# Where the early tiles of the FFN's `rest` lie, and where HGRN's modulation steps stand

## The chip, the cores and the metric

The kernel runs on one core of a Trainium2 chip. The metric is the device time of one execution in microseconds (us), the median of several runs. The engines are TensorE (PE in the profile; its weight loads are PEld), VectorE (DVE), ScalarE (ACT), GpSimd (POOL) and SyncE (SP, whose queue issues nearly all DMAs). Each engine works through its own instructions in a fixed order, and waits where an instruction's inputs or buffers are not ready.

## The reference, cut to what matters

A backbone of two layers on 512 latent tokens with 1024 features and 256 context tokens. Each layer is a half-step SwiGLU, a token mixer, and another half-step SwiGLU; each of these is modulated ahead and normalised behind:

```python
def modulate(x, m, k):
    return x * (1 + m[..., 3 * k + 1, :]) + m[..., 3 * k, :]
def post_norm_update(x, y, m, k, g, b):
    return layer_norm(DN_ALPHA * x + m[..., 3 * k + 2, :] * y, g, b)
def swiglu(h, w_in, w_out):
    gate, up = jnp.split(h @ w_in, 2, axis=-1)
    return (jax.nn.silu(gate) * up) @ w_out
```

The vectors m come from `silu(cond) @ w_mod + b_mod`, nine rows of 1024 for each layer. Layer 0's mixer is a bidirectional HGRN2 with 8 heads of 128: per head and direction a forget gate, a cumulative sum of its logarithm, scores inside chunks, states carried between chunks from the context's final state, and then `o * rsqrt(mean(o*o) + eps) * norm_w * silu(g)`, which goes to the output projection. Layer 1's mixer is a chunked spatial-gating MLP (CM).

## The kernel before, in words

**Matmuls.** Every fp32 operand is held as a high and a low part: `split` copies the high part on ScalarE (L136) and subtracts on VectorE (L137). `mm3` makes one product of three matmuls, high·high, high·low, low·high (L149 to L151). `unit` loads one block of weights (tile raw, three buffers, DMA on SP) and splits it into a tile w (six buffers).

**Stages.** f0 and f1 are the first FFN on latent and context tokens. Then come HGRN's values and heads (641 to 977 us in the trace), its output phase, f2 (second FFN of layer 0), f3 (first FFN of layer 1), CM, f4 (second FFN of layer 1) and the last output phase. An output phase (`OutPhase`) multiplies into y, and at the end of the stage makes the new x: it adds y times a gate row (L305, L307), takes statistics and normalises (L310, L315, L329; GpSimd makes the root, rstd), transposes x on PE (tile pt), scales it into the next stage's operand (L351) and splits that into xm. Between this and the first product of the next stage lies what is called the boundary here. Meanwhile it multiplies x by its norm weights (L296, L297; rows rg and rb from DRAM) and stores x to DRAM (L298); the next output phase loads it again (L360).

**f2, f3, f4.** `FeedSums` computes the two input halves of a SwiGLU block by a scheme with seven products on half-size operands in place of eight, on sums of operand parts (f5, f6, f4, f7) and of weight parts. `rest` runs over 20 blocks of 128 hidden features, in the order psc, pse, psc, psa, psc, pse, psc (banks in PSUM; 84 matmuls in each block). For each block it loads two weight blocks, raw and rawu (L561, L563), forms the weight sums e and changed rawu and raw by L572, L573, L574 and L576, splits the four, multiplies, keeps partial results in sc (ScalarE, L584), and combines them (L599 to L604). The first product needs only the split of raw; the second, into pse, needs e. The first blocks of f2, f3 and f4 are made during the boundary's tail from earlier units (psf; L485), and the rest in this loop.

**Where tiles lie.** Pools are opened and closed like a stack on the on-chip memory (SBUF). A tile that lies on bytes of a closed pool waits for the last readers and writers of the tiles that lay there before. So the place of a tile sets how early its DMA or its first instruction can be.

**HGRN.** For head h the order in the source is: forget gate of direction 0 (`proj_forget`: projections psfl and psfc, then a chain on VectorE and ScalarE that ends with Q, L890), the previous head's output transposes (`gated`: pto, L998, then ht, L1000), key transposes and scores of head h−1, forget gate of direction 1, states of head h−1 (S, Sc; L944 to L968), query projection (psq), and `outputs` of head h−1: product po from Sc and scores, squares (on), reduction to ss (L987, L988), a power on GpSimd (rs, L990), and on2 (L992), which the next `gated` transposes. Then the gate projection g.

**Modulation steps.** The 32 steps that make four rows of layer 1's modulation are spread through HGRN. A step loads 512 KB (tile mraw, two buffers, SP, L177) and multiplies it by the conditioning row in two instructions on VectorE (tile junk, L171), each with a read of its accumulator; after eight steps a reduction (L184) ends a row. `mod_step(n)` emits n steps, each with an edge that keeps it behind the instruction that `latest[0]` holds, which before is always the last split. A scheduler then orders each engine's instructions by its own estimates, within what the data and such edges allow.

Of the kernel before, what the change touches and what calls it, by code (L numbers as in the profile page):

```python
# [18 lines left out]
P = 128  # L19
D = 1024  # L20
# [50 lines left out]
def backbone_kernel(  # L71
# [433 lines left out]
    class FeedSums(FeedIn):  # L505
# [32 lines left out]
            add(self.f6, (1, 2), (0, 0))  # L538
            add(self.f7, (0, 2), (1, 2))

        def rest(self, hp, nmod=0):
            for f in range(len(self.pss) // 2):
                self.evac(hp, self.pss[2 * f], self.pss[2 * f + 1])
            K2, N2 = D // 2, 2 * P
            lo, hi = slice(0, K2), slice(K2, D)
            xm = self.xm
            b11, b21, b22 = (
                xm[:, :, k0 : k0 + KD // 2, c0 : c0 + N2] for k0, c0 in ((0, 0), (KD // 2, 0), (KD // 2, N2))
            )

            def product(ps, w, c0, b, start, stop):
                for k in range(KD // 2):
                    c = slice(c0 + k * P, c0 + (k + 1) * P)
                    mm3(
                        ps[:, :N2], (w[:, 0, c], w[:, 1, c]), (b[:, 0, k, :], b[:, 1, k, :]),
                        start and k == 0, stop and k == KD // 2 - 1, skip_group_check=True,
                    )

            for f in range(len(self.hs), NF):
                g = wpool.tile([P, D], F32, tag="raw", name="raw", bufs=3)  # L560
                nc.sync.dma_start(g, self.src(2 * f))  # L561
                u = hp.tile([P, D], F32, tag="rawu", name="rawu", bufs=2)
                nc.sync.dma_start(u, self.src(2 * f + 1))  # L563
                e = hp.tile([P, D], F32, tag="e", name="e", bufs=2)

                def weights(src, n=D):
                    w = wpool.tile([P, 2, D], F32R, tag="w", name="w", bufs=6)
                    split(w[:, 0, :n], w[:, 1, :n], src[:, :n])
                    return w

                wg = weights(g)
                nc.vector.tensor_tensor(e[:, lo], g[:, lo], u[:, lo], ALU.subtract)  # L572
                nc.vector.tensor_tensor(u[:, lo], u[:, hi], u[:, lo], ALU.subtract)  # L573
                nc.vector.scalar_tensor_tensor(e[:, hi], u[:, lo], -1.0, g[:, lo], ALU.mult, ALU.subtract)  # L574
                we = weights(e)
                nc.vector.scalar_tensor_tensor(g[:, lo], g[:, hi], -1.0, e[:, hi], ALU.mult, ALU.subtract)  # L576
                wu = weights(u)
                w4 = weights(g, K2)

                pc, pe, pa = bank("psc"), bank("pse"), bank("psa")  # L580
                sc = hp.tile([P, 4, N2], F32, tag="sc", name="sc", bufs=2)

                def kept(i, ps, scale=1.0):
                    nc.scalar.activation(sc[:, i, :], ps[:, :N2], AF.Copy, scale=scale)  # L584

                product(pc, wg, 0, b11, True, True)
                kept(0, pc)
                product(pe, we, 0, self.f5, True, True)
                kept(1, pe)
                product(pc, we, K2, self.f6, False, True)  # L590
                kept(2, pc)
                product(pa, wg, K2, b21, True, True)
                product(pc, wu, 0, self.f4, False, True)
                kept(3, pc, -1.0)
                product(pe, wu, K2, self.f7, False, True)
                product(pc, w4, 0, b22, False, True)
                s = hp.tile([P, T], F32, tag="silu", name="silu", bufs=1)
                h = hp.tile([P, T], F32, tag="h", name="h", bufs=NF)
                nc.vector.tensor_tensor(s[:, :N2], pa[:, :N2], sc[:, 0, :], ALU.add)  # L599
                nc.scalar.activation(s[:, :N2], s[:, :N2], AF.Silu)  # L600
                nc.vector.tensor_tensor(h[:, N2:], sc[:, 3, :], sc[:, 1, :], ALU.subtract)
                nc.vector.tensor_tensor(h[:, :N2], pe[:, :N2], sc[:, 2, :], ALU.add)
                nc.scalar.activation(s[:, N2:], pc[:, :N2], AF.Silu, scale=-1.0)
                nc.vector.tensor_tensor(h, h, s, ALU.mult)  # L604
                self.hs.append(h)
                mod_step(nmod)
                next(self.later, None)
            for _ in self.later:
                pass
            self.place.close()  # L610
            return lambda k: self.hs[k]
# [141 lines left out]
    with sbuf(name="hgo", bufs=1) as hgo, ExitStack() as late:  # L753
# [14 lines left out]
        with sbuf(name="hg", bufs=1) as hg:  # L768
# [81 lines left out]
            def proj_forget(h, d):  # L850
# [36 lines left out]
                    nc.vector.scalar_tensor_tensor(X3[:, s, :], B3[:, s, :], ref, X3[:, s, :], ALU.subtract, ALU.add)  # L887
                nc.scalar.activation(X, X, AF.Exp, scale=-1.0, bias=lnoml[:, i : i + 1])
                Q = B3[:, :NT, :]
                nc.vector.tensor_tensor(Q, Q, sm[:, :NT].unsqueeze(2).broadcast_to([P, NT, P]), ALU.subtract)  # L890
                nc.scalar.activation(Q, Q, AF.Exp)
                r.kk, r.Q, r.d = X3, Q, d
                return r, last
# [79 lines left out]
            def outputs(h, dirs):  # L973
# [15 lines left out]
                rs = hg.tile([P, NT, 1], F32, tag="rs", name="rs", bufs=2)  # L989
                nc.gpsimd.tensor_tensor(rs[:, :, 0], ss, neghalf[:, :NT], ALU.pow)  # L990
                on2 = hg.tile([P, NT, P], F32, tag="tmp", name="on2", bufs=3)
                nc.vector.tensor_tensor(on2, po3, rs.broadcast_to([P, NT, P]), ALU.mult)  # L992
                return on2

            def gated(h, on, g):
# [13 lines left out]
            for h in range(NH + 1):  # L1009
                if h == NH - NLATE + 2:  # L1010
                    late_outputs()
                mod_step(2 if h else 0)
                if h < NH:
                    n0, last = proj_forget(h, 0)
                else:
# [9 lines left out]
                    far_scores(0, r0)  # L1025
                if h == NH and 0 == 1:
                    gated(*done)
                mod_step(2 if h else 0)
                if h < NH:
                    n1, _ = proj_forget(h, 1)  # L1030
                if prev:
                    context_states(h - 1, prev, kTc)
                    kT1 = transposed([r1.kk[:, s, :] for s in lat_order(1)[:-1]])
                    latent_states(h - 1, 0, r0, kT0)
                    far_scores(1, r1)
                    latent_states(h - 1, 1, r1, kT1)
# [4 lines left out]
                else:  # L1041
                    if 0 == 2:
                        gated(*done)
                    op.lead(0, 2)
                mod_step(3 if h else 0)
                if prev:
                    on = outputs(h - 1, prev)
                    g, last = proj_silu(h - 1, 3, "g")
                    done = (h - 1, on, g)
                if h < NH:  # L1050
# [9 lines left out]
    L0.close()  # L1060


    with sbuf(name="hp2", bufs=1) as hp, bpools() as bp:
        hget = f2.rest(hp)
        xm = new_xm(xmp, "xm", T)
        f3 = FeedSums(
            1, 0, xm, NT,
# [5 lines left out]
        )  # L1073
        op.nhs = 8
        op.run(bp)
        hget = f3.rest(hp)
        xm = new_xm(xmp, "xm", T)

        class GateIn(Phase):
# [32 lines left out]
    with ExitStack() as vhp_stack:  # L1112
        vhp = vhp_stack.enter_context(sbuf(name="vh", bufs=NG + 1))
        hs = []
        bp = vhp_stack.enter_context(bpools())
        bw = []

        def new_block(i):
            if i % 3 == 0:
                bw.append(vhp.tile([P, NT, GC], F32, tag="vh", name="bw").rearrange("p t c -> p (t c)"))  # L1120
            return bw[-1][:, i % 3 * T : (i % 3 + 1) * T].rearrange("p (k t) -> p k t", k=2)

        f4 = FeedSums(1, 1, None, NT, new_block)
        op = OutPhase(
            lambda k: hs[k // 3][:, k % 3, :], CI // P, lambda hf, kk: cm_w_out[hf, kk], NT, 1, 1, "x", 1.0,
            lambda t: x4[t], True, (1, 2), None, lambda t: x5[t], f4, tail=3,
# [74 lines left out]
                hs.append(ht)  # L1201
        xm = new_xm(xmp, "xm", T)
        f4.xm = op.xm = xm
        op.run(bp)

    with sbuf(name="hp4", bufs=1) as hp, bpools() as bp:
        hget = f4.rest(hp)
        OutPhase(
            hget, NF, ffn_units(1, 1), NT, 1, 2, "x", 0.5, lambda t: x5[t], True, None,
            None, lambda t: out[t], None, tail=4,  # L1210
# [79 lines left out]
```

## Time and profile before

| | us |
|---|---|
| median of 3 runs | 2551.97 |
| lowest and highest | 2549.63, 2554.30 |
| the profiled execution's own time | 2548.07 |
| span of the profiled execution | 2546.4 |
| PE busy | 2449.6 (96%) |
| VectorE busy | 1887.0 (74%) |
| ScalarE busy | 1099.0 (43%) |
| mean granted PE clock | 0.987 of full speed |

How rows are read: in a timeline row stand the start, the duration, the engine, the line, the operation, out<-in, shapes and a count; brackets hold the idle time just before it and what ended it. A row of waits holds the total, the number and the longest. A row of windows holds the stretch, its length, busy time of PE, PEld, VectorE, ScalarE and GpSimd with the number of instructions, the granted PE clock, the share of DMA time and GB/s. SPq is SP's queue of DMA issues.

### The profile page before, as it was taken

The numbers are of one execution on the slowest core, as the hardware profiler recorded it, in microseconds if no ns is written. First come the engines' busy times: TensorE is split into PE (matmuls) and PEld (weight loads), VectorE is DVE, ScalarE is ACT, GpSimd is POOL, SyncE is SP. The second block draws the span as 40 slices with busy tenths as digits, with TensorE's granted clock in tenths as the row PEclk, the third lists the DMA queues.
The fourth block names the chain that finished last, engine by engine and source line by source line (L and its number), as shares of the span: only waits on it lengthen the run. The fifth ranks groups of instructions, "written<-read, shape, count | busy, mean of one in ns | idle before, by whom it ended". The sixth has DMA issues, their size and how long they took to land.

```text
span 2546.4 us, 37450 instructions
## 1 busy us (share of the span) xinstructions
PE 2449.6 (96%) x14687; PEld 2201.0 (86%) x14687; DVE 1887.0 (74%) x3361; ACT 1099.0 (43%) x1671; POOL 49.0 (2%) x82
## 2 busy tenths in 40 slices
PE   7999999999999999699999999998999999799998
PEld 5888889978888888699988999888998888699987
DVE  7965479783899986788756988657786346888765
ACT  4222434453444452455633555533332243455642
POOL 0000000000000000000000000000010000000001
PEclk9999999999999999899999999999999999899999
DMA  8866357973434213423432532325863223333332
GB/s 322 292 196 199 95 170 247 317 252 111 149 115 126 92 60 107 153 100 103 135 103 67 172 111 100 116 93 170 304 194 108 83 91 95 131 105 102 115 100 79
DMA packets 111170, 368.06 MB, mean 145 GB/s; under 512 B 12760, under 2 KB 16016, under 8 KB 110992
## 3 DMA queue, kind: packets, MB, share of 16 engines
q1 hardware_dynamic: 110992, 365.65, 43.3%
q8 instruction: 115, 1.88, 0.3%
q14 instruction: 63, 0.52, 0.1%
HBM read 352.99 MB, written 12.61 MB: 144 GB/s over the span
## 4 chain that ended last, share of the span: by engine, by line
PE 70%; DVE 17%; DMA 6%; ACT 3%; issue 2%; POOL 1%; SPq 0%; POOLq 0%; DVEq 0%; ACTq 0%
PE y L151 7%; PE y L150 7%; PE y L149 7%; PE psc L149 4%; PE psc L151 4%; PE psc L150 4%; PE psf L150 3%; PE psf L151 3%; PE psf L149 3%; DMA raw<-in_ffn_w_in 2%; DVE w L137 2%; PE pse L149 2%; PE pse L151 2%; PE pse L150 2%; DVE junk L171 2%
## 5 line engine op out<-in xcount | busy, mean ns | idle before, releaser
L137 DVE TENSOR_TENSOR w<-raw,w 128x1024 fp32r<-128x1024 f32 (+1 forms) x458 | 517.1, 1133 | 176.8 <-ACT w L136 175.0
L136 ACT ACTIVATE w<-raw 128x1024 fp32r<-128x1024 f32 (+1 forms) x458 | 449.9, 984 | 382.8 <-PE y L151 91.3
L149 PE MATMUL y<-w,hs 128*128 128x512 f32 x984 | 384.7, 391 | 2.3 <-ACT hs L136 2.2
L151 PE MATMUL y<-w,hs 128*128 128x512 f32 x984 | 384.4, 391 | 2.4 <-DVE hs L137 2.4
L150 PE MATMUL y<-w,hs 128*128 128x512 f32 x984 | 383.8, 390 | 0.0
L137 DVE TENSOR_TENSOR hs<-h,hs 128x512 fp32r<-128x512 f32 (+1 forms) x220 | 136.3, 636 | 151.6 <-ACT hs L136 151.6
L136 ACT ACTIVATE hs<-h 128x512 fp32r<-128x512 f32 (+1 forms) x220 | 126.1, 587 | 240.7 <-PE y L151 231.2
L151 PEld LDWEIGHTS y<-w,hs 128*128 128x128 f32 x984 | 185.2, 188 | 43.5 <-DVE hs L137 5.5
L149 PEld LDWEIGHTS y<-w,hs 128*128 128x128 f32 x984 | 185.2, 188 | 43.1 <-ACT hs L136 4.8
L150 PEld LDWEIGHTS y<-w,hs 128*128 128x128 f32 x984 | 185.1, 188 | 38.1
L149 PE MATMUL psf<-xm,w 128*128 128x512 f32 (+1 forms) x544 | 192.3, 360 | 19.8 <-ACT xm L136 19.3
L151 PE MATMUL psf<-xm,w 128*128 128x512 f32 (+1 forms) x544 | 193.6, 357 | 2.1 <-DVE w L137 2.1
L150 PE MATMUL psf<-xm,w 128*128 128x512 f32 (+1 forms) x544 | 194.1, 357 | 0.8 <-DVE xm L137 0.8
L171 DVE SCALAR_TENSOR_TENSOR junk<-mraw,srow_x 128x512 bf16<-128x512 f32 x256 | 167.0, 686 | 12.1 <-DMA mraw<-in_mod_w 11.9
L149 PE MATMUL pse<-f,w 128*128 128x256 f32 x480 | 137.3, 286 | 35.9 <-ACT w L136 35.9
L149 PE MATMUL psc<-f,w 128*128 128x256 f32 x480 | 136.9, 285 | 0.7 <-ACT sc L584 0.7
L151 PE MATMUL psc<-xm,w 128*128 128x256 f32 x480 | 136.1, 284 | 1.3 <-DVE w L137 1.3
L151 PE MATMUL pse<-f,w 128*128 128x256 f32 x480 | 137.3, 286 | 0.0
L150 PE MATMUL pse<-f,w 128*128 128x256 f32 x480 | 137.0, 285 | 0.0
L150 PE MATMUL psc<-f,w 128*128 128x256 f32 x480 | 136.5, 284 | 0.0
L151 PE MATMUL psc<-f,w 128*128 128x256 f32 x480 | 136.4, 284 | 0.0
L149 PE MATMUL psc<-xm,w 128*128 128x256 f32 x480 | 135.9, 283 | 0.0
(259 smaller groups left out, 5926.8 us busy)
## 6 DMA issues: line engine op xcount, KB each, us to landing
raw<-in_ffn_w_in SPq DMA_DIRECT2D x160, 512.0 KB, 4.5
mraw<-in_mod_w SPq DMA_DIRECT2D x144, 512.0 KB, 4.6
raw<-in_ffn_w_out SPq DMA_DIRECT2D x110, 512.0 KB, 3.6
rawu<-in_ffn_w_in SPq DMA_DIRECT2D x60, 512.0 KB, 3.5
raw<-in_hg_wf SPq DMA_DIRECT2D x32, 512.0 KB, 4.2
raw<-in_cm_wv SPq DMA_DIRECT2D x32, 384.0 KB, 4.0
raw<-in_cm_wu SPq DMA_DIRECT2D x24, 512.0 KB, 3.7
raw<-in_cm_w_out SPq DMA_DIRECT2D x24, 512.0 KB, 3.5
```

The costliest lines, as they stand in the source:

```text
L136: nc.scalar.activation(dst_hi, src, AF.Copy)
L137: latest[0] = nc.vector.tensor_tensor(dst_lo, src, dst_hi.bitcast(F32), ALU.subtract)
L149: nc.tensor.matmul(ps, ah, bh, start=start, stop=False, **kw)
L150: nc.tensor.matmul(ps, ah, bl, start=False, stop=False, **kw)
L151: return nc.tensor.matmul(ps, al, bh, start=False, stop=stop, **kw)
L171: nc.vector.scalar_tensor_tensor(junk, w[:, c], 1.0, s[:, c], ALU.mult, ALU.mult, dst[:, i : i + 1])
```

## The change

It has two parts.

First, `rest` takes rawu, e and sc (24 KB in all) from a pool of their own, sp2 for f2 and f3 and sp4 for f4, which is opened ahead of hp2 and hp4 and so lies lower in the stack. At f2 these bytes belonged to xmc, the context operand (rawu and e), and to the first heads' output tiles (sc); at f4 to buffers of CM's gate values. Before, the three lay behind silu and h in hp, on the output phase's x, t1 and row tiles and on the blocks bw. The blocks of f4 come from a new pool, bw4, in place of spare buffers of vh.

Second, in HGRN `latest[0]` is also set to Q's subtraction (L890) and to on2 (L992), and the steps of a head stand at two places: two behind the forget gate of direction 1, five behind `outputs`. Before they stood at three places (two, two and three), ahead of the forget gates and of `outputs`, and the edge was to the last split.

```diff
-        def rest(self, hp, nmod=0):
+        def rest(self, hp, sp, nmod=0):
...
-                u = hp.tile([P, D], F32, tag="rawu", name="rawu", bufs=2)
+                u = sp.tile([P, D], F32, tag="rawu", name="rawu", bufs=2)
...
-                e = hp.tile([P, D], F32, tag="e", name="e", bufs=2)
+                e = sp.tile([P, D], F32, tag="e", name="e", bufs=2)
...
-                sc = hp.tile([P, 4, N2], F32, tag="sc", name="sc", bufs=2)
+                sc = sp.tile([P, 4, N2], F32, tag="sc", name="sc", bufs=2)
...
-                nc.vector.tensor_tensor(Q, Q, sm[:, :NT].unsqueeze(2).broadcast_to([P, NT, P]), ALU.subtract)
+                latest[0] = nc.vector.tensor_tensor(Q, Q, sm[:, :NT].unsqueeze(2).broadcast_to([P, NT, P]), ALU.subtract)
...
-                nc.vector.tensor_tensor(on2, po3, rs.broadcast_to([P, NT, P]), ALU.mult)
+                latest[0] = nc.vector.tensor_tensor(on2, po3, rs.broadcast_to([P, NT, P]), ALU.mult)
...
             for h in range(NH + 1):
                 if h == NH - NLATE + 2:
                     late_outputs()
-                mod_step(2 if h else 0)
                 if h < NH:
                     n0, last = proj_forget(h, 0)
...
-                mod_step(2 if h else 0)
                 if h < NH:
                     n1, _ = proj_forget(h, 1)
+                mod_step(2 if h else 0)
...
-                mod_step(3 if h else 0)
                 if prev:
                     on = outputs(h - 1, prev)
+                    mod_step(5)
                     g, last = proj_silu(h - 1, 3, "g")
...
-    with sbuf(name="hp2", bufs=1) as hp, bpools() as bp:
-        hget = f2.rest(hp)
+    with sbuf(name="sp2", bufs=1) as sp, sbuf(name="hp2", bufs=1) as hp, bpools() as bp:
+        hget = f2.rest(hp, sp)
...
-        hget = f3.rest(hp)
+        hget = f3.rest(hp, sp)
...
-        f4 = FeedSums(1, 1, None, NT, new_block)
+        f4 = FeedSums(1, 1, None, NT, lambda i: bw.tile([P, 2, 2 * P], F32, name=f"bw{i}"))
...
+        bw = vhp_stack.enter_context(sbuf(name="bw4", bufs=1))
         op.run(bp)
 
-    with sbuf(name="hp4", bufs=1) as hp, bpools() as bp:
-        hget = f4.rest(hp)
+    with sbuf(name="sp4", bufs=1) as sp, sbuf(name="hp4", bufs=1) as hp, bpools() as bp:
+        hget = f4.rest(hp, sp)
```

What this does to the order of instructions is shown at three places. In the rows stand the line, the operation, out<-in and the shape.

SP's queue at the start of f2, before and of the change as one difference (x_84 is the store of x to DRAM; gr_8_x the gate row that the output phase behind f2 will use):

```order
 L234 DMA rgate<-gr_5_x 128x512
+L563 DMA rawu<-in_ffn_w_in 128x1024 x2
 L561 DMA raw<-in_ffn_w_in 128x1024
 L234 DMA rgate<-gr_8_x 128x512
-L298 DMA x_84<-x 128x512
-L234 DMA rg<-in_ln_g 128x512
-L234 DMA rb<-in_ln_b 128x512
-L298 DMA x_84<-x 128x512 x3
```

The first two loads of rawu stood behind eight stores of x and two loads of it; they now stand behind the second gate row of the phase before.

VectorE in the first evacuations and norms of the same boundary, as one difference:

```order
 L305 SCALAR_TENSOR_TENSOR t_9213<-y_9061,rgate 128x512
+L572 TENSOR_TENSOR e<-raw,rawu 128x512
 L307 TENSOR_TENSOR x<-x,t_9213 128x512
+L573 TENSOR_TENSOR rawu<-rawu 128x512
-L310 BN_STATS st<-x 128x6
-L315 BN_AGGR mv<-st 128x2
+L310 BN_STATS st<-x 128x6
+L305 SCALAR_TENSOR_TENSOR t_9224<-y_9062,rgate 128x512
+L315 BN_AGGR mv<-st 128x2
+L574 SCALAR_TENSOR_TENSOR e<-rawu,raw 128x512
 L329 TENSOR_SCALAR x<-x,mv,rstd 128x1024
```

The steps that form e, which stood behind the whole boundary, now stand between the evacuations that the first norms wait for; a second pair (L572, L573) follows before the second norm, and the split of e stands in the middle of the operand splits.

VectorE in HGRN around on2 of the fourth head; before:

```order
L831 TENSOR_TENSOR g_7603<-psq_7578,g_7603 128x512
L861 TENSOR_SCALAR X_7677<-psfl_7625 128x512
L137 TENSOR_TENSOR w_8009<-raw_8007,w_8009 128x1024
L171 SCALAR_TENSOR_TENSOR junk_7610,acc_x_7338<-mraw_7608,srow_x_5500 128x512
L171 SCALAR_TENSOR_TENSOR junk_7612,acc_x_7338<-mraw_7608,srow_x_5500 128x512
L987 TENSOR_REDUCE ss_7566<-on_7564 128x4
L171 SCALAR_TENSOR_TENSOR junk_7616,acc_x_7338<-mraw_7614,srow_x_5500 128x512
L988 TENSOR_SCALAR ss_7566<-ss_7566 128x4
L171 SCALAR_TENSOR_TENSOR junk_7618,acc_x_7338<-mraw_7614,srow_x_5500 128x512
L992 TENSOR_TENSOR on2_7571<-po_7551,rs_7569 128x512
```

And of the change, one head later, around on2 of the fifth:

```order
L831 TENSOR_TENSOR g_7993<-psq_7968,g_7993 128x512
L968 SCALAR_TENSOR_TENSOR S_7879<-pkl_7863,se_7385,S_7879 128x128
L137 TENSOR_TENSOR w_8009<-raw_8007,w_8009 128x1024
L962 TENSOR_SCALAR Sc_7882<-S_7879,se_7385 128x128
L137 TENSOR_TENSOR w_8126<-raw_8124,w_8126 128x1024
L137 TENSOR_TENSOR w_8273<-raw_8271,w_8273 128x1024
L137 TENSOR_TENSOR w_8336<-raw_8334,w_8336 128x1024
L987 TENSOR_REDUCE ss_7940<-on_7938 128x4
L988 TENSOR_SCALAR ss_7940<-ss_7940 128x4
L137 TENSOR_TENSOR w_8371<-raw_8369,w_8371 128x1024
L992 TENSOR_TENSOR on2_7945<-po_7925,rs_7943 128x512
L171 SCALAR_TENSOR_TENSOR junk_7949,acc_x_7548<-mraw_7947,srow_x_5500 128x512
```

The dots that stood ahead of on2 (L171) now follow it. The weight w_8009, which the projection psfl of the sixth head's direction 0 reads, was split a whole head ahead, beside the fourth on2; of the change it is split beside the fifth, behind g of that head.

More of the change, by code (lines that the diff above doesn't have):

```diff
@@ L1115, in backbone_kernel @@
         bp = vhp_stack.enter_context(bpools())
[L1116 to L1121, printed above, removed]
-        f4 = FeedSums(1, 1, None, NT, new_block)
+        f4 = FeedSums(1, 1, None, NT, lambda i: bw.tile([P, 2, 2 * P], F32, name=f"bw{i}"))
         op = OutPhase(
```

## The prediction

> **What bounds the kernel now.** The busy line of the page comes first: it says whose time the end is made of.
>
> ```profile
> PE 2449.6 (96%) x14687; PEld 2201.0 (86%) x14687; DVE 1887.0 (74%) x3361; ACT 1099.0 (43%) x1671; POOL 49.0 (2%) x82
> ```
>
> TensorE (PE) works for all but 97 of 2546.4 us, so a change gains only where PE stands still or runs slowly, and VectorE's 74% is a mean over stages. So the waits of PE by releaser are next (total, times, longest):
>
> ```profile
> PE pse L149 <- ACT w L136: 35.9, 2, 19.5
> PE pto L998 <- DVE on L992: 5.7, 4, 1.9
> PE po L981 <- DVE Sc L962: 2.6, 5, 1.0
> PE psc L151 <- DVE w L137: 1.3, 2, 1.1
> ```
>
> The first is two stalls, one at the start of each `rest`. The PE timeline has them, and those of VectorE and of the DMA queue (SP) what lies ahead:
>
> ```profile
> 1057.40 0.58 PE L149 MATMUL pse<-f,w 128*128 128x256 f32 x1 [19.52 <-ACT w L136]
> 2214.80 0.58 PE L149 MATMUL pse<-f,w 128*128 128x256 f32 x1 [16.38 <-ACT w L136]
> 1044.24 3.33 SPq L298 DMA_DIRECT2D x<-x  x4
> 1047.66 0.91 SPq L360 DMA_DIRECT2D x<-x  x2
> 1048.67 0.86 SPq L563 DMA_DIRECT2D rawu<-in_ffn_w_in  x2
> 1054.11 0.69 DVE L572 TENSOR_TENSOR e<-raw,rawu 128x512 f32<-128x512 f32 x1 [4.61 <-DMA rawu<-in_ffn_w_in]
> 1054.84 0.69 DVE L573 TENSOR_TENSOR rawu<-rawu 128x512 f32<-128x512 f32 x1
> 1057.38 1.23 DVE L137 TENSOR_TENSOR w<-e,w 128x1024 fp32r<-128x1024 f32 x1
> ```
>
> Read upwards: the second product waits for the weight that ScalarE and VectorE split from e; e waits for rawu; and rawu's loads leave SP only behind the stores of x, because its buffers lie on the out phase's tiles. PE has done the first product meanwhile and has nothing else.
>
> The stall is longer than its gap. The windows by stage (PE, PEld, DVE, ACT, POOL busy, then PE's granted clock) show what follows it:
>
> ```profile
> 1057.40:1062.20 4.80, 4.80 (x21) 4.68 (x22) 4.77 (x7) 2.75 (x4) 0.00 (x0) 0.50 0.24 74
> 1062.20:1067.00 4.80, 4.80 (x42) 4.80 (x41) 4.06 (x7) 3.48 (x6) 0.00 (x0) 1.00 0.35 144
> 2214.80:2220.00 5.20, 5.20 (x25) 5.08 (x26) 5.17 (x7) 2.75 (x4) 0.00 (x0) 0.56 0.88 317
> 839.90:844.20 4.30, 4.30 (x26) 4.30 (x25) 4.30 (x5) 3.86 (x6) 0.00 (x0) 0.60 0.75 232
> ```
>
> 4.80 us at half clock are 2.4 us lost (21 instructions, then 42 in as long), 5.20 at 0.56 are 2.3. The last row stands behind an HGRN wait of 1.89 us and loses 4.30 × 0.40 = 1.7.
>
> In HGRN the windows run from one head's output transposes (pto) to the next; below them the modulation dots (tile junk) alone, VectorE only:
>
> ```profile
> 641.00:718.20 77.20, 74.63 (x423) 64.97 (x422) 65.20 (x151) 37.72 (x54) 1.02 (x1) 1.00 0.42 137
> 718.20:758.50 40.30, 37.63 (x229) 32.84 (x227) 38.91 (x100) 19.89 (x30) 1.39 (x1) 1.00 0.37 123
> 758.50:798.80 40.30, 37.41 (x226) 32.75 (x227) 38.94 (x103) 19.19 (x29) 1.31 (x1) 1.00 0.44 141
> 798.80:839.40 40.60, 38.69 (x226) 34.60 (x227) 39.16 (x103) 19.30 (x29) 1.31 (x1) 0.96 0.46 142
> 839.40:878.20 38.80, 38.72 (x226) 34.47 (x227) 34.64 (x84) 18.21 (x28) 1.01 (x1) 0.96 0.27 82
> 641.00:718.20 77.20, 11.95 (x36) 1.00 0.42 137
> 758.50:798.80 40.30, 9.25 (x28) 1.00 0.44 141
> 839.40:878.20 38.80, 2.53 (x8) 0.96 0.27 82
> ```
>
> A step is four instructions (two dots, two reads of the accumulator), so 9.25 / 7 = 1.32 us; these stretches hold 9, 7 and 2 steps. In the three heads from 718 to 839 VectorE is the bound (38.91 of 40.30 busy). Before 718 and from 839 on PE is.
>
> **The change part by part: f2.** rawu, e and sc now lie on bytes that died before the boundary, and in the order of the change SP issues both rawu between the second gate row and x's stores. The whole stall goes: 19.5 + 2.4 = 21.9 us. f3, whose e already comes early, still has 1.3 us of waits for a weight split (the psc row above); I leave these in f2 and f4 too: 20.6.
>
> The e steps do not vanish; five of them and the split of e now stand among the first evacuations, norms and operand splits. The boundaries, from the first transposes to the first product of f2, f3 and f4:
>
> ```profile
> 1004.41:1036.28 31.87, 28.66 (x223) 28.06 (x224) 29.71 (x50) 15.83 (x26) 1.90 (x4) 0.95 0.06 22
> 1382.43:1412.28 29.85, 26.56 (x210) 26.30 (x210) 28.16 (x48) 16.03 (x28) 0.87 (x3) 0.94 0.12 39
> 2169.85:2196.83 26.98, 25.12 (x209) 24.89 (x209) 25.66 (x45) 15.83 (x26) 0.79 (x2) 1.00 0.05 21
> ```
>
> VectorE is 29.71 of 31.87 us busy at f2, so what is added there shows. Five steps at 0.61 (0.69 less the overlap with the next) are 3.1, the split of e 1.2 (1057.38), and the first step may wait for rawu's landing: 3.5 us from issue, and SP gets to it just ahead of the second gate row's work, so I take 0.9. Together 5.2, less half of the idle 2.16, which POOL's waits now covered give back: **4.1 lost**. Ends: none lost (all in idle time), or the 5.2 and another landing of 3.5, 8.7. f2 gains 20.6 − 4.1 = **16.5** (12 to 20).
>
> **f4.** The gap and the slow clock are 16.4 + 2.3 = 18.7, less f3's 1.3: 17.4. Six e steps (3.7) and two splits (2.4) enter the boundary, 6.1; held parts of y still keep PE at work there until the first transposes. f3's boundary, which has the same work in the same place, is 29.85 − 26.98 = 2.9 us longer than f4's: that row is the nearest, and I take **2.9** (0 to 6.1). f4 gains **14.5** (11 to 17). The new blocks' pool issues nothing, and its bytes died with the stage ahead. Late next, in both: the stores and reloads of x on SP and the later weights, which VectorE splits in time as in f3.
>
> **HGRN.** Nothing is removed: 32 steps stay, of which the stretch before 718 now holds 2 and the next ones 7, 7, 7, 7, 2. Each head has five steps behind on2 and two behind Q. What they covered is now bare, as it already is in the one head that has no dots ahead of its on2; then the queue's side of a step:
>
> ```profile
> 715.01 0.69 DVE L992 TENSOR_TENSOR on<-po,rs 128x512 f32<-128x512 f32 x1 [1.14 <-POOL rs L990]
> mraw<-in_mod_w SPq DMA_DIRECT2D x144, 512.0 KB, 4.6
> rawu<-in_ffn_w_in SPq DMA_DIRECT2D x60, 512.0 KB, 3.5
> ```
>
> Before 718: PE is 74.63 of 77.20 busy, so 9.2 us less on VectorE bring at most 2.6; I take −1. Heads 718 to 839: the same VectorE work, with 1.14 us of POOL's wait uncovered, and with two mraw buffers five steps in a row must fetch three anew, 4.6 us each, most of it behind the splits, additions and the scan that stand between them. Against that stand the pto waits (5.7 in four heads, plus 1.7 of slow clock behind each of two), gone or passed on to po, whose Sc now end the chain. I take +1.5 a head, +4.5. The fifth, 839 to 878: five steps more, 6.6 us; 34.64 + 6.6 = 41.2 busy, with the idle 1.4 of its neighbours 42.6, +3.8; besides, the lo half of its forget weight (w_8009) is split only behind g of the same head, while PE wants it in the third matmul after that head's psq: about 2 us more, and 1.7 of slow clock: +7.5 at most, taken **+6**. HGRN: −1 + 4.5 + 6 = **+9.5** (−6, if all pto and po waits go, to +17).
>
> Sum against the profiled run's own 2548.07: −16.5 − 14.5 + 9.5 = −21.5, so 2526.6. That run stands 3.9 us below the median of the three, 2551.97; on that scale it is **2530.5**.
>
> On the clock, the row behind the 19.5 us gap agrees with the Trainium skill, "TensorE: Matmul & The Clock Gate", section "Part 1: The HAM clock gate": half clock, though for 4.8 us instead of its 3.4 of sustained work. Its rule that an idle window of about 3.4 us is what throttles would give nothing for HGRN's short waits; the row behind 1.89 us idle (0.60 for 4.30 us) speaks against it. By that rule the fifth head would cost 1.7 less.
>
> **The rivals.** *HGRN costs nothing or gains* (place: the four heads with dots behind on2). For: 8.3 us of pto and po waits are on its chain, and two heads pay 1.7 us in clock. Against: VectorE has no room in three of them. HGRN at 0 to −6 gives −31 to −37: 2515 to 2521.
> *The stall moves instead of vanishing*: e steps, x's reloads, the banks of the third product take half of the 31 us; −15.5 + 9.5 = −6: 2546. For: VectorE has only 2.16 us idle at f2. Against: f3 does the same with 1.3 us of waits.
> *Slower: mraw bursts.* Place: the five steps behind on2, in four heads. If each step from the third on waits for a whole landing on VectorE (3 × 4.6 − 1.3 × 3 = 9.9 a head, and the weight splits queued behind it make PE wait), HGRN costs 40 + 9.5: 2570. It decides once HGRN loses more than 31 us. For: the queue holds seven mraw in one run, each waiting for a buffer. Against: between the dots stand splits, additions and a scan, so most of each landing is covered.
> *The bytes don't do what they are named for*: rawu still waits for a late reader at one of the two starts, which leaves −2 to −5 (2547 to 2550). The issue order, rawu ahead of x's stores, speaks against it.
>
> **How the numbers follow.** The forecast has 0.50, HGRN at no cost 0.24, the moved stall 0.13, slower by mraw 0.07, bytes 0.06. The forecast's own range: gains 23 to 37 and HGRN −1 to +16, so 2517 to 2546. The range for 8 in 10 reaches into the neighbours on both sides: 2515 to 2546. A measurement of this kernel tells about 0.2% (5.1 us): the first two cases are faster by more, of the third 0.06 is and 0.06 is within it, of the last 0.01 and 0.04: faster 0.81, within 0.2% 0.10, slower 0.09.
>
> **What would show it.** Right on f2 and f4: the groups "pse L149 <- ACT w" gone or under 3 us, rawu issued ahead of x's stores, both boundaries 3 to 5 us longer, and no half clock behind the first product. Right on HGRN: pto waits gone, po waits for Sc of 1 to 3 us, the fifth head above 42 us, the stretch before 718 a little shorter, the POOL wait ahead of on2 at 1.1. Wrong: mraw waits above 3 us a head; psfl waiting for a late split in other heads; heads under 40 us; a wait of PE for x, sc or a bank behind the first product of f2.

## The result, and the profile after

The changed kernel takes 2533.19 us (median of 4 runs, 2532.68 to 2538.23) against 2551.55 (4 runs) before: a ratio of 0.9932, 95% interval 0.9914 to 0.9949. The predicted time was 2530.5, with a range of 2515 to 2546. The profiled execution took 2532.92 us, with a span of 2531.2 against 2546.4.

The page's busy line of the changed kernel:

```profile
PE 2449.0 (97%) x14687; PEld 2199.0 (87%) x14687; DVE 1882.1 (74%) x3361; ACT 1100.1 (43%) x1671; POOL 49.3 (2%) x82
```

PE does the same work, so the 15.2 us of span came out of its idle and slow time. Its waits by releaser (total, times, longest):

```profile
PE psfl L151 <- DVE w L137: 7.1, 1, 7.1
PE pse L149 <- ACT silu L483: 6.9, 2, 3.8
PE pt L339 <- DVE x L329: 6.3, 4, 4.0
PE po L981 <- DVE Sc L962: 5.4, 6, 1.5
PE psc L151 <- DVE w L137: 4.0, 4, 1.5
PE pto L998 <- DVE on L992: 3.8, 4, 1.3
```

The row "pse <- ACT w" with its 35.9 us is gone. In its place stand five that were not there or were smaller: a weight split in HGRN (psfl, 7.1), silu at the start of both rests (6.9), the norms of f2's boundary (pt, 1.4 before), Sc (po, 2.6 before) and a weight split in the rests (psc, 1.3 before). pto fell from 5.7 to 3.8.

Where the time went, stage by stage. The lengths are differences between the starts of rows in the PE timeline (first psfl, the pto of each head, first pt, first and last row of psc, pse or psa):

| stretch | before | after | change |
|---|---|---|---|
| HGRN, first psfl to first pto | 70.1 | 68.1 | −2.0 |
| HGRN, first to last pto | 258.0 | 266.0 | +8.0 |
| last pto to f2's first pt | 27.9 | 29.2 | +1.3 |
| f2's boundary, first pt to first product | 32.1 | 35.0 | +2.9 |
| f2's rest | 224.4 | 207.6 | −16.8 |
| f3's rest | 203.5 | 203.5 | 0.0 |
| f4's boundary | 28.9 | 31.0 | +2.1 |
| f4's rest | 220.2 | 209.2 | −11.0 |

The rest of the difference (+1.8 ahead of HGRN, −1.1 in CM) is taken here as no effect of the change: over all runs, whose kernels have nearly the same code there, the first psfl starts between 644.9 and 650.0 us and CM takes 431 to 436. In a second profile of the changed kernel (below) the named stages repeat within 1 us, f2's boundary aside, which is 1.5 us longer. So stages tell more here than whole times do.

The two stalls in the PE timeline of the changed kernel, SP's first issues of rawu, and what VectorE and ScalarE do ahead of the first of the stalls:

```profile
1001.58 1.13 SPq L563 DMA_DIRECT2D rawu<-in_ffn_w_in  x2
1007.76 0.69 DVE L572 TENSOR_TENSOR e<-raw,rawu 128x512 f32<-128x512 f32 x1 [0.72 <-DMA rawu<-in_ffn_w_in]
1034.89 1.22 DVE L137 TENSOR_TENSOR w<-e,w 128x1024 fp32r<-128x1024 f32 x1
1060.46 1.06 ACT L136 ACTIVATE w<-e 128x1024 fp32r<-128x1024 f32 x1 [4.50 <-DVE e L574]
1062.48 1.28 ACT L483 ACT_TABLE_LOAD   x1
1063.78 0.60 ACT L483 ACTIVATE silu<-psf 128x512 f32<-128x512 f32 x1
1064.43 0.58 PE L149 MATMUL pse<-f,w 128*128 128x256 f32 x1 [3.10 <-ACT silu L483]
2209.93 0.58 PE L149 MATMUL pse<-f,w 128*128 128x256 f32 x1 [3.79 <-ACT silu L483]
```

rawu is issued at 1001.58, 47 us earlier than before, and e's split is ready 13 us before the first product ends. The second block's pse is what stalls now: it wants a PSUM bank that still holds the psf of the boundary, and silu, which empties it, comes only at 1063.78. ScalarE had stood idle for 4.50 us before it, waiting for the second block's e, whose split stands ahead of silu in its order.

HGRN by head, from pto to pto (length; busy PE, PEld, VectorE, ScalarE, GpSimd; granted clock):

```profile
717.97:759.64 41.67, 37.47 (x227) 33.00 (x227) 39.41 (x105) 20.19 (x30) 1.02 (x1) 1.00 0.41 129
759.64:799.53 39.89, 37.27 (x227) 32.83 (x227) 38.26 (x103) 18.34 (x28) 1.01 (x1) 1.00 0.42 132
799.53:839.32 39.79, 37.26 (x227) 32.82 (x227) 38.07 (x100) 18.48 (x28) 1.01 (x1) 1.00 0.41 131
839.32:884.98 45.66, 38.56 (x227) 34.37 (x228) 42.83 (x111) 20.38 (x30) 1.01 (x1) 0.93 0.48 150
```

The timeline around the one long wait:

```profile
871.26 0.68 DVE L831 TENSOR_TENSOR g<-psq,g 128x512 f32<-128x512 f32 x1
872.12 1.21 DVE L137 TENSOR_TENSOR w<-raw,w 128x1024 fp32r<-128x1024 f32 x1
873.39 0.80 PE L151 MATMUL psfl<-xm,w 128*128 128x512 f32 x1 [7.10 <-DVE w L137]
```

Three heads are together as long as before (121.4 us for 121.2); the fourth of these rows, 38.8 before, carries nearly the whole loss (the next head adds 1.0). No DMA wait stands at the split of the weight that psfl waits for; VectorE's order puts that split behind g.

### The profile page after: what moved, and what is told of

Read it like the earlier page. It is cut to its first block, busy times and chain, and to the rows that moved or that the text cites. A ratio compares the mean times of both kernels' runs of the same rounds, so it can differ in the third digit from the quotient of the medians.

```text
span 2531.2 us, 37425 instructions
## 1 busy us (share of the span) xinstructions
PE 2449.0 (97%) x14687; PEld 2199.0 (87%) x14687; DVE 1882.1 (74%) x3361; ACT 1100.1 (43%) x1671; POOL 49.3 (2%) x82
## 3 DMA queue, kind: packets, MB, share of 16 engines
q8 instruction: 115, 1.88, 0.3%
## 4 chain that ended last, share of the span: by engine, by line
PE 69%; DVE 17%; DMA 7%; ACT 3%; issue 2%; POOL 1%; SPq 0%; POOLq 0%; DVEq 0%; ACTq 0%
PE y L151 7%; PE y L149 7%; PE y L150 7%; PE psc L149 4%; PE psc L151 4%; PE psc L150 4%; PE psf L150 4%; PE psf L151 3%; PE psf L149 3%; DVE junk L171 2%; PE pse L149 2%; DVE w L137 2%; PE pse L151 2%; PE pse L150 2%; DMA raw<-in_ffn_w_in 2%
## 5 line engine op out<-in xcount | busy, mean ns | idle before, releaser
L171 DVE SCALAR_TENSOR_TENSOR junk<-mraw,srow_x 128x512 bf16<-128x512 f32 x256 | 165.7, 684 | 13.9 <-DMA mraw<-in_mod_w 13.9
```

Source lines behind the costliest of these rows:

```text
L171: nc.vector.scalar_tensor_tensor(junk, w[:, c], 1.0, s[:, c], ALU.mult, ALU.mult, dst[:, i : i + 1])
```

## The experiments

Eleven further runs were made, the last of them the changed kernel once more. One table for all, in us; "first" is first psfl to first pto, "heads" first to last pto, "to pt" the next stretch, b2 and b4 the boundaries of f2 and f4, r2 and r4 their rests. "span" is that of the profile, "time" the median; each ratio is to runs of the kernel before that were made together with that row's runs, not to the first row:

| kernel | first | heads | to pt | b2 | r2 | b4 | r4 | span | time | ratio to before, interval |
|---|---|---|---|---|---|---|---|---|---|---|
| before | 70.1 | 258.0 | 27.9 | 32.1 | 224.4 | 28.9 | 220.2 | 2546.4 | 2551.55 | |
| changed | 68.1 | 266.0 | 29.2 | 35.0 | 207.6 | 31.0 | 209.2 | 2531.2 | 2533.19 | 0.9932 [0.9914, 0.9949] |
| changed, again | 68.1 | 266.3 | 29.6 | 36.5 | 207.1 | 30.8 | 208.8 | 2533.4 | 2534.59 | 0.9931 [0.9918, 0.9944] |
| pools alone | 71.1 | 257.8 | 29.9 | 36.5 | 207.1 | 31.4 | 210.1 | 2534.0 | 2531.99 | 0.9924 [0.9906, 0.9941] |
| HGRN alone | 68.1 | 267.2 | 27.9 | 31.6 | 223.4 | 28.9 | 219.6 | 2550.4 | 2554.0 | 1.0008 [0.9998, 1.0017] |
| from head 0 | 74.0 | 267.6 | 30.0 | 35.0 | 206.9 | 31.2 | 209.6 | 2538.6 | 2538.53 | 0.9945 [0.9927, 0.9963] |
| early silu | 68.1 | 268.1 | 29.8 | 35.0 | 204.7 | 30.9 | 202.9 | 2520.8 | 2529.44 | 0.9908 [0.9891, 0.9926] |
| late e | 68.1 | 266.6 | 27.9 | 33.2 | 210.1 | 30.4 | 211.3 | 2537.1 | 2539.1 | one run |
| unit ahead | 68.1 | 274.5 | 29.8 | 35.0 | 207.1 | 31.1 | 209.4 | 2541.6 | 2543.28 | one run |
| two gate rows | 68.1 | 266.4 | 27.9 | 34.9 | 206.7 | 30.8 | 208.8 | 2526.8 | 2528.52 | one run |
| three together | 68.1 | 274.7 | 27.9 | 34.3 | 203.9 | 31.2 | 203.9 | 2528.8 | 2533.71 | 0.9928 [0.9909, 0.9947] |
| old HGRN, rest best | 70.1 | 258.0 | 27.9 | 34.0 | 203.9 | 31.3 | 203.4 | 2518.1 | 2520.76 | 0.9878 [0.9864, 0.9891] |
| six steps a head | 69.7 | 253.6 | 27.9 | 34.8 | 203.9 | 31.3 | 203.3 | 2511.9 | 2510.54 | 0.9842 [0.9828, 0.9855] |

**Each part alone.** The pools alone are the changed kernel with this edit; HGRN alone is the kernel before with the same lines the other way round:

```diff
-                latest[0] = nc.vector.tensor_tensor(Q, Q, sm[:, :NT].unsqueeze(2).broadcast_to([P, NT, P]), ALU.subtract)
+                nc.vector.tensor_tensor(Q, Q, sm[:, :NT].unsqueeze(2).broadcast_to([P, NT, P]), ALU.subtract)
-                latest[0] = nc.vector.tensor_tensor(on2, po3, rs.broadcast_to([P, NT, P]), ALU.mult)
+                nc.vector.tensor_tensor(on2, po3, rs.broadcast_to([P, NT, P]), ALU.mult)
...
+                mod_step(2 if h else 0)
                 if h < NH:
                     n0, last = proj_forget(h, 0)
...
+                mod_step(2 if h else 0)
                 if h < NH:
                     n1, _ = proj_forget(h, 1)
-                mod_step(2 if h else 0)
...
+                mod_step(3 if h else 0)
                 if prev:
                     on = outputs(h - 1, prev)
-                    mod_step(5)
```

> The change's first part alone (own pools for rawu, e, sc and for f4's blocks); HGRN's steps stand where they stood before. Theory (the two parts add, and HGRN's is a loss): f2's and f4's rest lose their 19.5 and 16.4 us gaps as in the changed kernel, HGRN from the first pto to the last takes 258 us as before instead of 266; about 2529 minus 3, that is 2526 to 2530, 7 to 8 us under the changed kernel. Rival (the longer HGRN is only work that f2's boundary would wait for anyway): about 2533, with the 7.7 us back as a longer boundary.

> The change's second part alone (HGRN's steps behind Q and on2; tiles lie as before). Theory: HGRN 7 to 8 us longer, nearly all of it in the fifth head, whose psfl waits about 7 us for the low half of its weight; about 2559. Rival (the steps' new places cost nothing by themselves, and the wait needs the other pools' loads on the queue): 2550 to 2553.

In the stages both came out as the theory had it: the pools alone leave HGRN at 71.1 + 257.8 and take the stalls; HGRN alone has the same 7.1 us wait of psfl and the heads 9.2 us longer, the stretch before them 2.0 shorter. In the whole times they did not. The pools alone are 1 us under the changed kernel, not 7 to 8. Their profile does have HGRN 5.2 us shorter, but CM, which has the same code in both, took 436.4 us in it against 431.2; and each of the two medians is uncertain by about 4.5 us. HGRN alone is 2 us over the kernel before (interval −0.5 to +4.3), where its two HGRN stages together are 7.2 longer in the trace. That profile's span is 4.0 longer; the other 3 us came off ahead of HGRN, in f2 and in f4, stages that this part does not touch. So: the part costs 6 to 7 us in its own stages; what it costs the whole is between nothing and 4 by these runs, and the gap between the two is not settled.

**HGRN from head 0.** Two and five steps in head 0 too:

```diff
-                mod_step(2 if h else 0)
+                mod_step(2)
                 if prev:
...
                 if prev:
                     on = outputs(h - 1, prev)
-                    mod_step(5)
+                mod_step(5)
+                if prev:
                     g, last = proj_silu(h - 1, 3, "g")
```

> The changed kernel, with HGRN's steps started one head earlier: two and five steps in head 0 too, so that the stretch before the first pto has nine of them, as before the change, and the fifth head none behind on2. Theory A (the fifth head loses because five more steps and a late weight split meet there, and the first stretch has room on VectorE): the 7.1 us wait of psfl is gone, HGRN about 258 us, 2525 to 2528. Theory B (each head with dots behind on2 and seven mraw loads ahead of the weights' loads drifts later, and the last of them pays): the wait of 5 to 7 us stands one head earlier, 2531 to 2534.

This is theory B, and worse than it: the wait of psfl is still 7.09 us, now two heads earlier, the heads are within 2 us of the changed kernel's, and the first stretch, which has nine steps again but behind Q and on2, is 5.9 longer than the changed kernel's. The head that waits now had seven steps before the change too. So the wait needs neither five additional steps nor that one head; it goes with the arrangement.

**The weight one place earlier.** To ask whether the order of one split on VectorE is the cause, the next head's direction-0 weight is loaded and split ahead of the two steps behind Q:

```diff
+            ready = {}
...
-                w = unit(hg_wf[1 + d, h])
+                w = ready.pop((h, d), None) or unit(hg_wf[1 + d, h])
...
                     n1, _ = proj_forget(h, 1)
+                    if h and h + 1 < NH:
+                        ready[h + 1, 0] = unit(hg_wf[1, h + 1])
                 mod_step(2 if h else 0)
```

> The changed kernel, with the next head's direction-0 weight loaded and split one place earlier, ahead of the two steps behind Q. Theory (the 7.1 us wait of psfl is an order on VectorE: the split stands behind g of the same head, though its data landed long before): the wait is gone and HGRN from first to last pto is 258 to 261 us instead of 266. Rival (VectorE has no room in that head, so another late thing takes its place): a wait of 4 us or more elsewhere in the same head (for Sc, q or another split), HGRN 264 or more.

The waits of PE for the states (Sc, and the keys kT for their product pkl) in this kernel, and behind them two of its heads as windows:

```profile
PE po L982 <- DVE Sc L964: 11.4, 3, 4.3
PE pkl L960 <- ACT kT L908: 5.6, 3, 2.8
```

```profile
758.31:802.23 43.92, 38.94 (x226) 34.02 (x227) 39.57 (x104) 19.41 (x30) 1.01 (x1) 0.96 0.42 132
802.23:846.72 44.49, 39.51 (x226) 34.57 (x227) 39.31 (x101) 19.36 (x30) 1.01 (x1) 0.92 0.41 131
```

The rival came true: the 7.1 us wait is gone, and waits for Sc of 4.3, 4.3 and 2.8 us take its place in three heads; HGRN is 8.5 us longer still. The split was what PE waited for; with it moved ahead, VectorE is late with the states.

**silu and the first h early.** They lay in hp2 and hp4; now they too come from sp2 and sp4:

```diff
...
-                self.evac(hp, self.pss[2 * f], self.pss[2 * f + 1])
+                self.evac(sp, self.pss[2 * f], self.pss[2 * f + 1], "h0", 2)
...
-                s = hp.tile([P, T], F32, tag="silu", name="silu", bufs=1)
-                h = hp.tile([P, T], F32, tag="h", name="h", bufs=NF)
+                s = sp.tile([P, T], F32, tag="silu", name="silu", bufs=1)
+                h = hp.tile([P, T], F32, tag="h", name="h", bufs=NF - 2)
...
```

> The changed kernel, with silu and the first two h of f2, f3 and f4 also in the early pools (6 KB more of them; h in the loop has two buffers fewer), so that the first banks can be emptied before x's second half. Theory A (the 3.1 and 3.8 us waits of pse for silu come from where these tiles lie, which puts their instructions behind the second block's splits): these waits gone, f2's rest 203.5 to 205 us instead of 207.6, f4's 203.5 to 206 instead of 209.2, about 2525. Theory B (the second block would wait for its weights or sums at that place anyway): a wait of 2 to 4 us for w or e stands there instead, 2531 to 2534.

From its ScalarE and VectorE timeline in f2:

```profile
1043.92 0.60 ACT L483 ACTIVATE silu<-psf 128x512 f32<-128x512 f32 x1 [1.08 <-PE psf L151]
1047.40 0.69 DVE L485 TENSOR_TENSOR h<-psf,silu 128x512 f32<-128x512 f32 x1
```

Theory A came true. silu runs 2 us before the first product (1045.88) instead of 15.6 behind it, no wait of pse for silu is left, and the rests are 204.7 and 202.9, near f3's 203.5; the median, 2529.4, lies 4 us above the forecast. What the runs don't show is why the scheduler held silu back. In the changed kernel no wait on the old place's bytes stands in front of silu, and ScalarE idled 4.50 us for the second block's e just ahead of it: it is the order on ScalarE that the place of these tiles changed. Whether silu could have run earlier at its old place is not shown.

**The e steps late.** Tiles early, but the steps held behind the boundary's last operand split:

```diff
+            nxt.tail = last
             nxt.sums()
...
-                nc.vector.tensor_tensor(e[:, lo], g[:, lo], u[:, lo], ALU.subtract)
-                nc.vector.tensor_tensor(u[:, lo], u[:, hi], u[:, lo], ALU.subtract)
-                nc.vector.scalar_tensor_tensor(e[:, hi], u[:, lo], -1.0, g[:, lo], ALU.mult, ALU.subtract)
+                with tc.issue_after(self.tail.ins):
+                    nc.vector.tensor_tensor(e[:, lo], g[:, lo], u[:, lo], ALU.subtract)
+                    nc.vector.tensor_tensor(u[:, lo], u[:, hi], u[:, lo], ALU.subtract)
+                    nc.vector.scalar_tensor_tensor(e[:, hi], u[:, lo], -1.0, g[:, lo], ALU.mult, ALU.subtract)
```

> The changed kernel, with the e steps of f2, f3 and f4 (L572 to L574) held behind the boundary's last operand split: the tiles lie early, only the steps are late. It prices the term of the boundary. If the 4.2 us by which f2's boundary grew are the e steps' place on VectorE: from the last pto to the first product 60 to 62 us instead of 64.2, and pse then waits 4 to 7 us for the split of e, so the stage as a whole is 0 to 4 us longer than the changed kernel's; if the loads beside the gate row make the boundary longer, its first transposes stay as late as in the changed kernel (29.2 us behind the last pto) and only what follows them shortens.

From the last pto to f2's first product 61.2 us instead of 64.2 (60.0 before), and f2's rest 2.5 longer: the same sum. The first transposes came at 27.9 although rawu was loaded as in the changed kernel, so the steps held them up and the loads alone do not. In f3, whose e steps had always been early, the edit shows what the late place costs. Its VectorE and PE timelines there (L576 is the step that is L574 in the changed kernel):

```profile
1404.92 1.90 DVE L296 SCALAR_TENSOR_TENSOR x<-x,rg 128x512 f32<-128x512 f32 x3 [0.66 <-DMA rg<-in_ln_g]
1407.30 1.90 DVE L297 SCALAR_TENSOR_TENSOR x<-rb,x 128x512 f32<-128x512 f32 x3 [0.49 <-DMA rb<-in_ln_b]
1409.72 0.68 DVE L576 SCALAR_TENSOR_TENSOR e<-rawu,raw 128x512 f32<-128x512 f32 x1
1411.55 0.58 PE L149 MATMUL pse<-f,w 128*128 128x256 f32 x1 [8.67 <-ACT w L136]
```

f3's rest grew from 203.5 to 213.1: x's multiplications by its norm weights now stand between the e steps on VectorE. In f3 the early place is the cheaper one; in f2 the two cost the same.

**Two gate rows.**

```diff
+RG = ((0, 1, 'x'),)
...
-            self.gate = load_row(self.bp, "rgate", made((self.l, 3 * self.j + 2, self.cond))[0, c])
+            self.gate = load_row(self.bp, "rgate", made((self.l, 3 * self.j + 2, self.cond))[0, c], bufs=2 if (self.l, self.j, self.cond) in RG else 1)
```

> The changed kernel, with two buffers for the gate row of f2's output phase, so that its second row is loaded ahead of raw and rawu. Theory (of the 1.3 us by which the first transposes come later, the gate row's slower landing beside rawu is the cause: VectorE waited 2.60 us for it, 0.82 before the change): that wait is gone and the first transposes come 26.5 to 28 us behind the last pto instead of 29.2, the whole 1.5 to 2.5 us shorter. Rival (the e steps and rawu's own landing hold VectorE there): 28.5 us or more.

The first transposes come after 27.87 us, as before the change; f2 takes from the last pto to the end of rest 269.4 instead of 271.8. In its VectorE timeline the evacuation that waited 2.60 us for the row (L305, here L306) waits for nothing, and the e steps fit in:

```profile
1001.07 0.68 DVE L306 SCALAR_TENSOR_TENSOR t<-y,rgate 128x512 f32<-128x512 f32 x1
1001.96 0.69 DVE L573 TENSOR_TENSOR e<-raw,rawu 128x512 f32<-128x512 f32 x1 [0.21 <-DMA rawu<-in_ffn_w_in]
```

Together with the run of the late steps: there the same evacuation was as late as in the changed kernel (22.7 us behind the last pto; 22.4 there, 20.6 before the change), yet the first transposes came at 27.9. So they are late only when the steps and a late gate row meet, and the theory's cause is half of it. Each of these two runs is a single one.

**Together, and the best.** Early silu, the unit ahead and two gate rows in one kernel:

> The changed kernel with three edits together: silu and the first h in the early pools, the direction-0 weight one place earlier in HGRN, two buffers for the gate row. If the terms add: 9 us less in f2 and f4, 5 to 8 less in HGRN, 2 less at the boundary, about 16 us under the changed kernel, 2514 to 2520. If they share their covers, 2522 to 2528.

Neither forecast came true (2533.7): HGRN is as long as with the unit alone (274.7), the other terms add. Then the old HGRN order with early silu and two gate rows, and the same with one step fewer a head; the changed kernel ran beside them:

```diff
-                mod_step(3 if h else 0)
+                mod_step(2 if h else 0)
                 if prev:
                     on = outputs(h - 1, prev)
```

> HGRN's steps as before the change, the pools of the change, silu and the first h in the early pools too, two buffers for f2's gate row. If the terms of the earlier runs add: HGRN from the first psfl to the last pto 328.9 us as in the kernel before (the changed kernel 334.1), f2 from the last pto to the end of rest 27.9 + 35 to 36 + 204 us, f4's boundary and rest 235; 5 to 10 us under the kernel with the early silu alone on the same chip state, 2519 to 2525. If HGRN's old order lengthens f2 by more than the 1.7 us it did in the run of the pools alone, 2526 to 2530.

> The same with two steps instead of three ahead of outputs, so six a head instead of seven, and the last steps in later heads, where VectorE has room (31.3 of 37.5 us busy). Theory (in three heads VectorE is the bound at 38.9 of 40.3 us, and a step is 1.32 us): those heads about 1 us shorter each, the fifth at most 1 longer, HGRN 1 to 3 us shorter than in the run with seven, 2517 to 2523. Rival (the chain through Sc, po, on2 and pto sets a head's length whatever VectorE's load): heads at 40.2 to 40.6 as before, no difference.

> The changed kernel itself, on the chip and in the rounds of the two others, so that they are compared on one scale: 2531 to 2536; from first psfl to last pto 334 us, f2's rest 207.6 with pse's 3.1 us wait for silu, f4's 209.2 with its 3.8.

The old order gives 2520.8, 14 us under the changed kernel beside it, and six steps a head 2510.5, 24 under it and 40 under the kernel before. The heads with seven steps in the old order, then with six:

```profile
720.14:760.43 40.29, 37.59 (x228) 32.77 (x226) 38.90 (x100) 19.90 (x30) 1.39 (x1) 1.00 0.41 125
800.78:841.35 40.57, 38.67 (x227) 34.57 (x227) 39.14 (x103) 19.29 (x29) 1.31 (x1) 0.96 0.45 140
```

```profile
717.63:756.05 38.42, 37.34 (x228) 32.83 (x227) 37.28 (x96) 18.85 (x29) 1.02 (x1) 1.00 0.37 115
795.04:833.94 38.90, 37.38 (x227) 32.86 (x227) 38.10 (x99) 18.95 (x29) 1.01 (x1) 1.00 0.43 133
```

One step less on VectorE makes a head 1.4 to 1.9 us shorter (a step is 1.32), so VectorE's load sets these heads, as the theory had it; the one pto wait that is left is 0.3 us, and those of pkl for ScalarE are 0.8 to 1.2. The fifth head, which now has six steps instead of two, did not grow (38.8). The gain in the whole, 10.2 us between the two medians, took the time below its forecast of 2517 to 2523 and is more than the 4.8 that HGRN shows; the surplus lies in stages that differ between profiles, and is not explained.

## Why the prediction was right, and where it was not

The forecast was the net of two stalls removed and HGRN lengthened: −21.5 us, 2530.5. It came out as −15.2 in the profiled span and −18.4 in the medians. That the sum is this near is in part luck: f2 and f4 gained 21.5 us net of their boundaries instead of 31.0, which lies below the forecast's own 23 to 37 (f4's 8.9 lies outside its 11 to 17), and HGRN cost 6.0 instead of 9.5, which gave a third of that back. By its own steps:

- **"The whole stall goes", f2: 20.6, and f4: 17.4.** Too large: the rests lost 16.8 and 11.0. The stall did go, and the place of rawu on the queue was the cause, as predicted. What the term left out is the next late thing. I wrote that the stores, reloads and later weights come "late next" but in time "as in f3". f3 was the wrong model for one step: there silu and the first h lie on free bytes, and here they were ordered behind the second block's splits. The trace has 3.1 and 3.8 us of waiting there and slow clock behind; by the run with the early silu the whole is worth 2.9 (207.6 − 204.7) and 6.3 (209.2 − 202.9). This is the rival "the stall moves", in a small form. With these taken away the rests stand near f3's length, and the rest of the term was sized rightly: 19.7 and 17.3.
- **"4.1 lost" at f2's boundary and 2.9 at f4's.** Right: 1.3 + 2.9 = 4.2, and 2.1; the second profile of the changed kernel has 1.7 + 4.4 = 6.1 at f2, so the agreement there is closer than the measurement. The parts of the 4.1 were not all right: the landing of rawu cost 0.72 where I took 0.9, and a part that I had not seen, the gate row that lands later beside it, joins it (the two-gate-row run took 1.3 off).
- **Before 718: −1.** −2.0, inside its bound of 2.6.
- **Heads 718 to 839: +4.5.** Wrong: +0.2. I let 1.14 us of bared wait for GpSimd's power and the mraw landings add to a full VectorE. The wait for the power was there before as well, although dots stood ahead of on2. VectorE's waits in these heads, before and after:

```profile
DVE on L992 <- POOL rs L990: 2.7, 3, 0.9
DVE on L992 <- POOL rs L990: 3.5, 3, 1.2
```

So 0.3 us a head was uncovered and not 1.14. On PE the waits of po and pkl grew by 3.0 and 0.7 us in the three heads; pto's fell by 1.8, and the slow clock behind one of them, which had cost 1.7, did not come (1.00 where it had been 0.96).
- **The fifth head: +6**, with a late lo half of its weight. Right in mechanism: the order showed the split behind g, and the trace has 7.10 us on it. The size, +6.8, came out by luck: I had put about 2 us on the wait itself and 3.8 on five more steps, and the wait alone is as long as the whole growth; the run from head 0 has the same wait in a head that had seven steps before the change too. The stretch also held nearly nine steps and not seven (11.44 us of dots): the two that I had put into the next one fell ahead of its end. The next head's +1.0 is not in the forecast.
- **The rivals.** "HGRN costs nothing or gains" and "slower by mraw bursts" are both out: HGRN lost 6.0 us, and VectorE's waits for mraw in the heads from 718 to 840 come to 0.8 us. That the bytes don't do what they are named for is out by the issue time of rawu.
- **The signs.** rawu's early issue, the stall's end and the shorter stretch before 718 came as signs of being right. The half clock behind the start of the rests (below) and pto waits of 3.8 us remained, and two signs of being wrong appeared: heads under 40 us, and a wait of PE for a bank behind the first product of f2.
- **The clock.** Behind waits of 3.10, 3.79 and 7.10 us the granted clock in the changed kernel was:

```profile
1064.40:1069.00 4.60, 4.57 (x27) 4.57 (x28) 4.60 (x10) 3.63 (x7) 0.00 (x0) 0.67 0.87 265
2209.90:2214.50 4.60, 4.57 (x22) 4.57 (x23) 4.18 (x8) 1.81 (x5) 0.00 (x0) 0.52 1.01 395
873.40:878.00 4.60, 4.60 (x25) 4.41 (x26) 2.48 (x4) 1.18 (x2) 0.00 (x0) 0.69 0.66 207
```

That is 1.4 to 2.2 us lost behind each, near the prediction's 1.7 to 2.4. The Trainium skill, "TensorE: Matmul & The Clock Gate", section "Part 1: The HAM clock gate", has only full and half clock for this gate; by that, 0.67 over 4.6 us is half clock for 3.0 of them: near its 3.4 us of work that lift the throttle. Its 3.4 us of idleness that set it are too long for this kernel: 1.89 us were enough in the kernel before, while waits of up to 1.5 us in the changed kernel's heads left 1.00.

## What to carry to other kernels

When a stall at a stage's start comes from where a tile lies, list every tile that the first two blocks of the stage write, the small ones that empty a bank too: moving three of five here left a shorter stall behind the first. Where the helper engine is the bound of a stage, its work per period is what counts: six pieces in each of five periods were faster here than the orders of seven in four that were tried. And judge an edit by its own stage, since whole times of one kernel here differed by 5 to 10 us from run to run.

## What the runs showed of the hardware that was not expected

In HGRN's heads the granted clock did not fall behind PE waits of 1.1 to 1.6 us, and fell behind both waits of 1.89 us in the kernel before (0.60 for 4.3 us behind the second). But length alone does not decide it. In the run of the pools alone, waits of 1.88 us (ended at 801.40) and 1.90 us (841.61) came out differently:

```profile
801.40:805.70 4.30, 4.30 (x33) 4.08 (x34) 4.29 (x6) 4.05 (x6) 0.00 (x0) 1.00 0.71 222
841.61:845.91 4.30, 4.30 (x24) 4.30 (x25) 4.16 (x5) 3.32 (x5) 0.00 (x0) 0.60 0.69 242
```

So a wait near 1.9 us cost either nothing more or another 1.7 us (4.30 × 0.40); what decides between the two is not shown.

The gate row, 256 KB of one row spread to all partitions, took 5.2 us from issue to use beside four loads of 512 KB (issue at 1001.20, use at 1006.35) and 3.4 before the change with two of them on the way (993.45 to 996.82).
